# One more modulation unit summed on VectorE, attention transposes one step later, and the output norm written in pieces, in a two-layer fp32 diffusion step

## The chip, the cores and the metric

The kernel runs on one core of one Trainium2 chip. The metric is the device time of one execution in microseconds (us): the median of three runs is 2344.78 us, from 2342.45 to 2346.54. Matrix products run on TensorE (PE; its weight loads are shown as PEld), elementwise work on VectorE (DVE), activations and copies on ScalarE (ACT), a little on GpSimd (POOL); SyncE (SP) only issues transfers.

## The reference, cut to what matters

Two groups of 128 tokens, a prompt and a sample (256 columns in all), go through two layers with D = 2048. Each layer is a mixer and a gated MLP with a width-3 convolution, each behind a norm that is shifted, scaled and gated by six vectors per layer, which are themselves a product of a condition with a weight matrix (`w_ada`, 2048 by 12288 for each layer):

```python
def _trunk(x, cond, ...):
    for l in range(DEPTH):                                   # 2 layers
        mod = jax.nn.silu(cond) @ w_ada[l] + b_ada[l]        # (1, 6 * 2048)
        sh1, sc1, gt1, sh2, sc2, gt2 = jnp.split(mod[:, None, :], 6, axis=-1)
        h = rmsnorm(x, g_norm_mix[l]) * (1 + sc1) + sh1
        m, new = mixer_ab(h, ...) if l % 2 == 0 else mixer_c(h, ...)
        x = x + gt1 * m
        h = rmsnorm(x, g_norm_ffn[l]) * (1 + sc2) + sh2
        x = x + gt2 * conv_ffn(h, w_ffn_up[l], w_ffn_conv[l], b_ffn_conv[l], w_ffn_down[l])
    return rmsnorm(x, g_final), ab_ctx, c_ctx

def softmax_attention(q, k, v, scale):                       # 16 heads of mixer_ab: 8 "mla", 8 "gqa"
    s = jnp.einsum("bqhgd,bkhd->bhgqk", qb, k) * scale
    p = jax.nn.softmax(s, axis=-1)
    return jnp.einsum("bhgqk,bkhd->bqhgd", p, v)
```

The prompt group reads its own 128 keys, the sample group those and 128 cached ones. All is float32.

## The kernel before, in words

**Tokens lie in the columns**: `x` is 16 chunks of 128 features by 256 tokens and stays in SBUF for the whole run. The weights stream through once, in transfers of 1 MB into tiles called `raw` (three buffers) that SyncE issues in order. To multiply float32 data the kernel splits each weight into a rounded part `wh` (a cast on ACT, L222) and a rest `wl` (a subtraction on DVE, L223), and does the same to the activations. One 128x128 block is then three matmuls of 256 columns (L339 wh with the high part, L340 wh with the low part, L343 wl with the high part), which accumulate in a PSUM bank `acc` (three of them).

**The modulation vectors** are made beside this, from `w_ada`, which streams in tiles of 1 MB called `araw` (two buffers, also issued by SyncE). A unit (l, j, q) is a quarter (512 outputs) of vector j of layer l and takes four such tiles. The list `ROWS` gives the order of units. Most are done on TensorE (`sum_rows`, L453): for each tile four fp32 matmuls of 32x512, at the end a copy `am` on ACT (L395), four transposes (L402), a reduction on DVE (L404) and the bias (L412). Units whose index is in `SUMMED` are done on VectorE (`feature_sum`, L430): two multiplies with a sum over 128x2048 for each tile, eight for a unit; their products go to a `junk` tile that nobody reads, and their order against the work around them is fixed. A second list, `FEATS`, holds units that are always done on VectorE.

**The order** is written out as demands. After each chunk of weights `pump()` is called: it advances the list of units by a rate (`RATE`, `row_step`), and `step()` advances every attention head by one `yield`, since a head is a generator (`head_ab`). A scheduler then places each engine's instructions by its own estimates, within the dependencies.

**The stages by the trace**, in us from the start of the span: first norm and the input projection of the first mixer (0 to 211); its heads, with the query and key/value up-projections (211 to about 351); its output projection with the gated residual (L618; 351 to 447); MLP, second mixer, MLP (447 to 2330); last norm and output (2330 to 2343.7). In the heads a head is: scores (L666, into one of three banks `att`), softmax parts (maxima and scale on DVE, exponentials on ACT), scaling by the reciprocal (L674, L675), a yield, three transposes and the copy `pT` on ACT (`transposed`, L656 and L658), a yield, and the product with the values (L680 to L682), which is split into `hx` chunk c, the input of the output projection.

**A later norm** (`stat_add`, `stat_rstd`) is the tail of each stage: the residual of the last chunk on DVE (L618), its square on ACT (L173), two matmuls for each group (L202 on the sum of the other squares, L203 on the last square), a power on POOL (L189), a diagonal (L209) and its spread over the partitions by a matmul (L217). The last norm is followed by 16 multiplications (L1156) and four output transfers (L1159).

Of the kernel before, what the change touches and what calls it, by code (L numbers as in the profile page):

```python
# [12 lines left out]
BF16 = mybir.dt.bfloat16  # L13
AF = mybir.ActivationFunctionType
ALU = mybir.AluOpType
# [3 lines left out]
P = 128  # L19
# [59 lines left out]
FEATS += [(1, 5, 1), (1, 5, 2), (1, 5, 3)]  # L79
RLIMIT = {"ab": 18, "ffn0": 19, "c": 30, "ffn1": 31}  # L80
FLIMIT = {"ab": 2, "ffn0": 14, "c": 14, "ffn1": 17}
SUMMED = [20, 21, 22, 24, 25, 26, 29]
INV = {2048: 0, 768: 1, 512: 2, 128: 3, 256: 4}


# [1 line left out]
def step_kernel(ctx: ExitStack, tc: tile.TileContext, A: dict):  # L87
# [22 lines left out]
    def T_(pl, shape, tag, dt=F32, bufs=None):  # L110
        kw = {} if bufs is None else {"bufs": bufs}
        return pl.tile(shape, dt, tag=tag, name=nm(tag), **kw)
# [41 lines left out]
    def start(g):  # L154
        if next(g, chains) is not chains:
            chains.append(g)
# [8 lines left out]
    def stat_add(st, src, n):  # L165

        st["n"] += 1
        if st["n"] == 1:
            st["acc"] = T_(keep, [P, NT], "sqacc")
            act.activation(st["acc"], src, AF.Square)  # L170
            return
        sq = T_(tmp, [P, NT], "sq", bufs=2)
        act.activation(sq, src, AF.Square)  # L173
        if st["n"] == n:
            st["last"] = sq
        else:
            pool.tensor_tensor(out=st["acc"], in0=st["acc"], in1=sq, op=ALU.add)  # L177

    def rstd(cols, n, factor=1.0, out=None):
# [247 lines left out]
    def feature_sum(unit, t, c, raw, junk):  # L427

        l, j, q = unit
        tc.keep_in_program_order(dve.tensor_tensor_reduce(  # L430
            out=junk, in0=raw, in1=condb[:, c].rearrange("p (g n) -> p g n", g=4), scale=1.0, scalar=0.0,
            op0=ALU.mult, op1=ALU.add, accum_out=mod[:, l, j, 4 * q + t, c:c + 1]))
# [25 lines left out]
    def row_step(until=len(ROWS)):  # L458
        if later:
            later.pop(0)()  # L460
        if ada["i"] >= until:
            return
        l, j, q = ROWS[ada["i"]]
        if ada["i"] < 8:
            return pair_step(l, j, q)
        t, g = divmod(ada["t"], 4)
        on_dve = ada["i"] in SUMMED
        if g == 0:
            ada["raw"] = T_(wpool, [P, 4, 512], "araw", bufs=2)
            sp.dma_start(out=ada["raw"], in_=A["w_ada"][l, j, q, t])  # L470
        raw = ada["raw"]
        if on_dve:
            if g % 2:
                feature_sum((l, j, q), t, g // 2, raw, T_(ada["pool"], [P, 4, 512], "junk", BF16, bufs=1))
        elif pinned[0]:
            if g == 1 and t:
                sum_rows(t - 1, ada["last"])
            if g == 3:
                ada["last"] = raw
                if t == 3:  # L480
                    last = ada["last"]
                    later.append(lambda: None)
                    later.append(lambda: sum_rows(3, last))
        elif g == 3:
            sum_rows(t, raw)
        ada["t"] += 1
        if ada["t"] == 16:
            later.extend([lambda: biased(l, j, q)] if on_dve else ada_finish(l, j, q))
            ada["i"] += 1
            ada["t"] = 0  # L490
# [162 lines left out]
    def transposed(pl, p, bufs=2):  # L653
        pt = T_(ppool["att"], [P, 512], "att", bufs=3)
        for b in range(3):
            pe.transpose(pt[:, b * T:(b + 1) * T], p[:, b * T:(b + 1) * T], ident)  # L656
        o = T_(pl, [P, 3 * T], "pT", bufs=bufs)
        act.copy(o, pt[:, :3 * T])  # L658
        return o

    def head_ab(pl, pairs, rs, v, hx, c):

        s = T_(ppool["att"], [P, 512], "att", bufs=3)
        for g, ks in ((0, slice(0, T)), (1, slice(T, 3 * T))):
            for i, (q, k) in enumerate(pairs):
                pe.matmul(s[:, ks], q[:, g * T:(g + 1) * T], k[:, ks],  # L666
                          start=(i == 0), stop=(i == len(pairs) - 1))
        mx = T_(small, [P, 2], "mx")
        sums = T_(small, [P, 2], "sums")
        p = T_(pl, [P, 3 * T], "p", bufs=2)  # L670
        softmax_parts(s, mx, sums, rs, None, p)
        rec = T_(small, [P, 2], "rec")
        dve.reciprocal(out=rec, in_=sums)
        dve.tensor_scalar(out=p[:, :T], in0=p[:, :T], scalar1=rec[:, 0:1], scalar2=None, op0=ALU.mult)  # L674
        dve.tensor_scalar(out=p[:, T:], in0=p[:, T:], scalar1=rec[:, 1:2], scalar2=None, op0=ALU.mult)  # L675
        yield
        pT = transposed(pl, p)
        yield
        o = T_(ppool["att"], [P, 512], "att", bufs=3)
        pe.matmul(o[:, 0:T], v(0), pT[:, 0:T], start=True, stop=True)  # L680
        pe.matmul(o[:, T:NT], v(1), pT[:, T:2 * T], start=True, stop=False)
        pe.matmul(o[:, T:NT], v(2), pT[:, 2 * T:], start=False, stop=True)  # L682
        split(hx[:, c, :NT], hx[:, c, NT:2 * NT], o[:, :NT])


    def mixer_ab(hx, rb0, st):
        l = 0
        with tc.tile_pool(name="ab", bufs=1) as ab:
# [158 lines left out]

            with tc.tile_pool(name="abh", bufs=1) as hp:
                ada["pew"] = PEW["heads"]

                o = T_(keep, [P, KD, ROW], "hx", F32R)
                load_cw(0)
# [31 lines left out]
                for h in range(0, 8, 2):  # L884
                    for i in range(2):
                        ps = gemm(WQ.chunk(), qh, qlo)
                        qn[i] = T_(hp, [P, NT], "qn", bufs=3)
                        act.copy(qn[i], ps)
                        pump(RATE["heads"])
                    ps = gemm(WQ.chunk(), qh, qlo)  # L890
                    ev = T_(tmp, [P, NT], "nt", bufs=4)
                    act.copy(ev, ps)
                    qr = T_(hp, [P, NT], "qr", bufs=2)
                    act.copy(qr[:, 0:T], ev[:, 0:T])
                    rope(qr[:, None, T:], ev[:, None, T:], 1, 32, "rcm", "rsm")
                    pump(RATE["heads"])
                    kn = []
                    for i in range(2):
                        if h + i < 7:
                            start(gqa_query(h + i + 1))  # L900
                        start(gqa(h + i))
                        ps = gemm(WK.chunk(), kh, klo, 3 * T)
                        kn.append(T_(hp, [P, 3 * T], "kn", bufs=2))
                        act.copy(kn[i], ps)
                        pump(RATE["heads"])
                    wide = WK.pieces
                    WK.blocks = []
                    vm = T_(hp, [P, 3, 2, P], "vm", bufs=1)
                    vs = vm.rearrange("p b i d -> p (b i d)")
                    two, one = T_(pacc, [P, 512], "acc"), T_(pacc, [P, 512], "acc")  # L910
                    for xs, out in zip(tokens, (two[:, :NT], two[:, NT:], one[:, :NT])):
                        by_token(wide, xs, [out], True, True)
                    act.copy(vs[:, :2 * NT], two)
                    act.copy(vs[:, 2 * NT:], one[:, :NT])
                    pump(RATE["heads"])
                    start(mla(h, qn[0], qr, kn[0], vm))
                    pump(RATE["heads"])
                    start(mla(h + 1, qn[1], qr, kn[1], vm))
# [137 lines left out]
    def ffn(hx, W, ready, todo, l, st):  # L1056
# [4 lines left out]
        with tc.tile_pool(name=f"ffn{l}", bufs=1) as fp, banks(f"pffn{l}") as pf:  # L1061
# [38 lines left out]
            def down(gs, q):  # L1100
                for c in range(KD):
                    quiet = q == NQ - 1 and c >= KD - QUIET[0]
                    fine[0] = quiet
                    ps = gemm(WD.chunk(), lambda k: gs[k][:, :NT], lambda k: gs[k][:, NT:2 * NT])
                    residual(ps, l, 1, c, st if q == NQ - 1 else None)
                    pump(0, 0 if quiet else FRATE["down"])

            for q in range(NQ):
# [29 lines left out]
    ffn(hx, W, ready, todo, 0, st)  # L1138
    stage[0] = "c"
    with tc.tile_pool(name="cc", bufs=1) as cp, banks("pc") as ppool["ada"]:  # L1140
        ada["pool"] = cp
        ppool["att"] = ppool["ada"]
        W = Weights(A["w_in_c"], KD, 1)
        hx, ready, todo = modulated(st, 1, 0, W, True)
        load_cw(1)
        st = stat_init()
        ada["pew"] = PEW["c"]
        mixer_c(cp, hx, W, ready, todo, st)
        W = Weights(A["w_up"][1], KD, 1)
        hx, ready, todo = modulated(st, 1, 1, W, True)  # L1150
# [1 line left out]
    st = stat_init()  # L1152
    ffn(hx, W, ready, todo, 1, st)
    rb = norm_scale(st)
    for c in range(KD):
        dve.scalar_tensor_tensor(out=x[:, c], in0=x[:, c], scalar=C("gfin")[:, c:c + 1], in1=rb,  # L1156
                                 op0=ALU.mult, op1=ALU.mult)
        if c % 4 == 3:
            sp.dma_start(out=A["o_y"][:, c - 3:c + 1], in_=x[:, c - 3:c + 1])  # L1159

# [132 lines left out]
```

## Time and profile before

| | |
|---|---|
| median of three runs | 2344.78 us (2342.45 to 2346.54) |
| the profiled execution's own time | 2345.51 us |
| its span on the core | 2343.7 us |
| granted TensorE clock, mean | 0.993 of full speed |
| busy share of the span | PE 98%, DVE 78%, ACT 50%, POOL 6% |
| moved by DMA | 610.81 MB, 261 GB/s on average |

The span runs from the first to the last instruction of the core; what lies between it and the execution's own time is 1.8 us. PE is busy nearly throughout, so a time that is saved or added must show as PE work, as an idle stretch of PE, or at the two ends of the span, where PE has nothing to do.

### The profile page before, as it was taken

Reading aid. Unit: us, or ns where it says so; the run is one execution under the profiler, and the core shown is the slowest. Engines: PE = TensorE matmul, PEld = TensorE weight load, DVE = VectorE, ACT = ScalarE, POOL = GpSimd, SP = SyncE. Lnnn points to the kernel's source line nnn. Section 1 sums busy time; section 2 is a strip of 40 time slices with the busy share of each in tenths; the row PEclk is TensorE's granted clock in tenths of the full one; section 3 lists DMA queues with packets and bytes.
Section 4 is the critical chain, followed back from the end, with each engine's and each line's share of the span. In section 5 each row is a group of like instructions: output and inputs, shape, how many; then the busy total and the mean of one; then the engine's idle time right before and its main releaser. Section 6 shows DMA issues by size and latency. Waiting matters only on the chain. (4 is left out here: it accounts for less than half of the span.)

```text
span 2343.7 us, 47002 instructions
## 1 busy us (share of the span) xinstructions
PE 2295.5 (98%) x19582; PEld 2189.7 (93%) x19582; DVE 1817.6 (78%) x2692; ACT 1162.2 (50%) x1833; POOL 144.9 (6%) x133
## 2 busy tenths in 40 slices
PE   7999999999999999999999999999999999999997
PEld 6788878799999999999989999898999999999997
DVE  3667558879999999999869889887899755666654
ACT  4346554555553355554465555446555434555542
POOL 0002001200000000001220000022000000000011
PEclk9999999999999999999999999999999999999998
DMA  9996779777767777777767788786677555555553
GB/s 386 338 360 257 264 280 376 285 263 259 261 256 288 292 267 267 270 260 271 280 235 265 267 308 301 285 325 228 234 261 264 195 198 196 189 193 197 198 190 117
DMA packets 92421, 610.81 MB, mean 261 GB/s; under 512 B 9968, under 2 KB 17840, under 8 KB 20528
## 3 DMA queue, kind: packets, MB, share of 16 engines
q1 hardware_dynamic: 92208, 607.80, 70.3%
q8 instruction: 154, 2.52, 0.4%
q14 instruction: 59, 0.48, 0.1%
HBM read 603.01 MB, written 4.75 MB: 259 GB/s over the span
## 5 line engine op out<-in xcount | busy, mean ns | idle before, releaser
L222 ACT CAST wh<-raw 128x1024 fp32r<-128x1024 f32 (+1 forms) x788 | 793.2, 1012 | 936.6 <-PE acc L340 756.1
L223 DVE TENSOR_TENSOR wl<-raw,wh 128x1024 fp32r<-128x1024 f32 (+1 forms) x788 | 923.1, 1186 | 318.1 <-ACT wh L222 306.9
L339 PE MATMUL acc<-hx,wh 128*128 128x256 f32 x3808 | 1058.7, 279 | 6.3 <-ACT hx L569 4.6
L340 PE MATMUL acc<-hx,wh 128*128 128x256 f32 x3808 | 1055.9, 278 | 0.6 <-DVE hx L554 0.6
L343 PE MATMUL acc<-hx,wl 128*128 128x256 f32 x3808 | 1056.0, 278 | 0.0
L339 PEld LDWEIGHTS acc<-hx,wh 128*128 128x128 f32 x3808 | 716.0, 188 | 32.4 <-issue 9.2
L343 PEld LDWEIGHTS acc<-hx,wl 128*128 128x128 f32 x3808 | 716.0, 188 | 7.9 <-issue 6.7
L340 PEld LDWEIGHTS acc<-hx,wh 128*128 128x128 f32 x3808 | 716.8, 188 | 3.8 <-issue 2.6
L430 DVE CUSTOM_DVE_ANT_0 junk<-araw,condb 128x2048 f32<-128x2048 f32 (+1 forms) x192 | 442.9, 2307 | 0.1
L340 PE MATMUL acc<-g,wh 128*128 128x256 f32 x1408 | 388.3, 276 | 0.0
L343 PE MATMUL acc<-g,wl 128*128 128x256 f32 x1408 | 388.0, 276 | 0.0
L339 PE MATMUL acc<-g,wh 128*128 128x256 f32 x1408 | 387.8, 276 | 0.0
L340 PEld LDWEIGHTS acc<-g,wh 128*128 128x128 f32 x1408 | 264.3, 188 | 0.0
L343 PEld LDWEIGHTS acc<-g,wl 128*128 128x128 f32 x1408 | 264.2, 188 | 0.0
L339 PEld LDWEIGHTS acc<-g,wh 128*128 128x128 f32 x1408 | 264.1, 188 | 0.0
L177 POOL TENSOR_TENSOR sqacc<-sqacc,sq 128x256 f32<-128x256 f32 x62 | 84.9, 1369 | 1575.2 <-issue 1293.8
L1071 ACT ACTIVATE cv<-acc,convw 128x256 f32<-128x256 f32 x176 | 98.2, 558 | 1.4 <-PE acc L327 1.4
L618 DVE SCALAR_TENSOR_TENSOR x<-acc,mod,x 128x128 f32<-128x128 f32 x192 | 58.0, 343 | 42.5 <-PE acc L343 41.7
L1077 DVE SCALAR_TENSOR_TENSOR cv<-acc,convw,cv 128x254 f32<-128x254 f32 x176 | 84.3, 479 | 3.6
L1074 DVE SCALAR_TENSOR_TENSOR cv<-acc,convw,cv 128x254 f32<-128x254 f32 x176 | 83.5, 475 | 2.5 <-ACT cv L1071 2.5
L453 PE MATMUL ada<-araw,condw 128*32 128x512 f32 x512 | 68.6, 603 | 4.2 <-DMA araw<-w_ada 4.2
L304 PE MATMUL acc<-wh,hx 128*128 128x256 f32 x256 | 70.3, 281 | 0.9 <-ACT dv L982 0.9
(238 smaller groups left out, 2127.5 us busy)
## 6 DMA issues: line engine op xcount, KB each, us to landing
araw<-w_ada SPq DMA_DIRECT2D x178, 1024.0 KB, 5.5
raw<-w_up SPq DMA_DIRECT2D x176, 1024.0 KB, 4.8
raw<-w_down SPq DMA_DIRECT2D x88, 1024.0 KB, 4.8
raw<-w_in_c SPq DMA_DIRECT2D x48, 1024.0 KB, 5.6
raw<-w_in_ab SPq DMA_DIRECT2D x19, 1024.0 KB, 7.2
raw<-w_out_ab SPq DMA_DIRECT2D x16, 1024.0 KB, 7.4
raw<-w_out_c SPq DMA_DIRECT2D x16, 1024.0 KB, 6.0
condb<-w_ada SPq DMA_DIRECT2D x12, 1024.0 KB, 7.1
```

The costliest lines, as they stand in the source:

```text
L177: pool.tensor_tensor(out=st["acc"], in0=st["acc"], in1=sq, op=ALU.add)
L222: pin(act.copy(out_hi, src))
L223: pin(dve.tensor_tensor(out=out_lo, in0=src, in1=out_hi.bitcast(F32), op=ALU.subtract))
L304: pe.matmul(ps, hi, wh[:, s], start=a, stop=False)
L339: fixed(pe.matmul(ps[:, :n], wh, xh(k), start=(i == 0), stop=False))
L340: fixed(pe.matmul(ps[:, :n], wh, xl(k), start=False, stop=False))
L343: fixed(pe.matmul(ps[:, :n], wl, xh(k), start=False, stop=(i == last)))
L430: tc.keep_in_program_order(dve.tensor_tensor_reduce(out=junk, in0=raw, in1=condb[:, c].rearrange("p (g n) -> p g n", g=4), scale=1.0, scal ...
L453: i = pe.matmul(ada["ps"][32 * g:32 * g + 32, :], condw[:, 4 * t + g, :], raw[:, g], start=(t == 0), stop=(t == 3), skip_group_check=True)
L1071: pin(act.activation(y, ps, AF.Identity, scale=cw[:, 1, m:m + 1], bias=cw[:, 3, m:m + 1]))
L1074: pin(dve.scalar_tensor_tensor(out=y3[:, :, 1:], in0=p3[:, :, :T - 1], scalar=cw[:, 0, m:m + 1], in1=y3[:, :, 1:], op0=ALU.mult, op1=ALU.add))
L1077: pin(dve.scalar_tensor_tensor(out=y3[:, :, :T - 1], in0=p3[:, :, 1:], scalar=cw[:, 2, m:m + 1], in1=y3[:, :, :T - 1], op0=ALU.mult, op1=A ...
```

## The change

It has four parts.

1. Index 10 joins `SUMMED`: this is unit (0, 2, 2), a quarter of the first mixer's gate, whose four tiles are streamed while the heads run. Its eight sums are now done on VectorE. The heads have no space for a junk tile, so the products go to chunks 4 to 7 of `o`, which is the first mixer's `hx` and not yet written there (`ada["junk"]`, set to None at h = 4, before the first of those heads starts). The unit's weights come transposed, as those of the other units in `SUMMED` do.
2. `head_ab` has one more `yield` ahead of `transposed`: in all 16 heads the transposes of the attention weights come one demand later, and what follows them too.
3. At the end, the multiplication by `g_final` moves into the last down-projection, as an activation with a scale on ACT after each chunk's residual; what is left after the norm are five multiplications of 2, 4, 4, 4 and 2 chunks, each followed by its own output transfer, in place of 16 and four.
4. The last square of each norm behind the first stage (three of them: ahead of the second mixer, ahead of the second MLP, and at the end) is done in two halves, one for each group of tokens.

```diff
-SUMMED = [20, 21, 22, 24, 25, 26, 29]
+SUMMED = [10, 20, 21, 22, 24, 25, 26, 29]
@@ stat_add
         sq = T_(tmp, [P, NT], "sq", bufs=2)
-        act.activation(sq, src, AF.Square)
         if st["n"] == n:
+            for s in ([slice(0, NT)] if stage[0] == "ab" else [slice(0, T), slice(T, NT)]):
+                act.activation(sq[:, s], src[:, s], AF.Square)
             st["last"] = sq
         else:
+            act.activation(sq, src, AF.Square)
             pool.tensor_tensor(out=st["acc"], in0=st["acc"], in1=sq, op=ALU.add)
@@ row_step
-                feature_sum((l, j, q), t, g // 2, raw, T_(ada["pool"], [P, 4, 512], "junk", BF16, bufs=1))
+                feature_sum((l, j, q), t, g // 2, raw, ada["junk"]())
@@ head_ab
         yield
+        yield
         pT = transposed(pl, p)
         yield
@@ the heads
                 ada["pew"] = PEW["heads"]
+                ada["junk"] = lambda: o[:, 4:8]
...
                     pump(RATE["heads"])
+                    if h == 4:
+                        ada["junk"] = None
                     start(mla(h, qn[0], qr, kn[0], vm))
@@ down
                     residual(ps, l, 1, c, st if q == NQ - 1 else None)
+                    if l == 1 and q == NQ - 1:
+                        act.activation(x[:, c], x[:, c], AF.Identity, scale=C("gfin")[:, c:c + 1])
                     pump(0, 0 if quiet else FRATE["down"])
@@ the second mixer
-        ada["pool"] = cp
+        ada["junk"] = lambda: T_(cp, [P, 4, 512], "junk", BF16, bufs=1)
@@ the end
     rb = norm_scale(st)
-    for c in range(KD):
-        dve.scalar_tensor_tensor(out=x[:, c], in0=x[:, c], scalar=C("gfin")[:, c:c + 1], in1=rb,
-                                 op0=ALU.mult, op1=ALU.mult)
-        if c % 4 == 3:
-            sp.dma_start(out=A["o_y"][:, c - 3:c + 1], in_=x[:, c - 3:c + 1])
+    for c, n in ((0, 2), (2, 4), (6, 4), (10, 4), (14, 2)):
+        dve.tensor_tensor(out=x[:, c:c + n], in0=x[:, c:c + n], op=ALU.mult,
+                          in1=rb[:, None, :].to_broadcast([P, n, NT]))
+        sp.dma_start(out=A["o_y"][:, c:c + n], in_=x[:, c:c + n])
```

Line numbers after the change are higher by two behind `stat_add`, and by up to seven towards the end (L430 becomes L432, L656 L658, L666 L668, L680 L683).

Two places in the heads show what moves. The first is VectorE in the first quarter of the heads, around a head's softmax (its `p` scaled by L674 and L675) and the next pieces of split weights (`wl`). Before:

```order
L673 RECIPROCAL rec_2593<-sums_2585 128x2
L674 TENSOR_SCALAR p_2586<-p_2586,rec_2593 128x128
L675 TENSOR_SCALAR p_2586<-p_2586,rec_2593 128x256
L223 TENSOR_TENSOR hx_2381<-att_2612,hx_2381 128x256
L223 TENSOR_TENSOR wl_2789<-raw_2782,wh_2788 128x512
L404 TENSOR_REDUCE mod_77<-ada_2571 128x8
L412 TENSOR_TENSOR mod_77<-mod_77,cst_74 128x8
L223 TENSOR_TENSOR wl_2887<-raw_2884,wh_2886 128x1024
L223 TENSOR_TENSOR wl_2891<-raw_2884,wh_2890 128x1024
```

And the same place after:

```order
L677 TENSOR_SCALAR p_2582<-p_2582,rec_2589 128x256
L432 ISA hx_2381,mod_77<-araw_2502,condb_82 128x2048
L432 ISA mod_77 128x1
L225 TENSOR_TENSOR wl_2769<-raw_2762,wh_2768 128x512
L225 TENSOR_TENSOR hx_2381<-att_2669,hx_2381 128x256
L644 TENSOR_REDUCE mx_2690<-att_2685 128x1
L645 TENSOR_REDUCE mx_2690<-att_2685 128x1
L406 TENSOR_REDUCE mod_77<-ada_2566 128x8
L649 SCALAR_TENSOR_TENSOR nmx_2693<-mx_2690,rsmla_240 128x2
L414 TENSOR_TENSOR mod_77<-mod_77,cst_74 128x8
L432 ISA hx_2381,mod_77<-araw_2502,condb_82 128x2048
L432 ISA mod_77 128x1
```

Two of the eight sums (each is an instruction of 128x2048 and a short one that writes its result) now stand there, the first ahead of the pieces of weights `wl` and the second ahead of the next ones; the maxima of the next head, which came later, stand between them.

The second place is TensorE ahead of the second pair of heads' value up-projection (the `L304` product; `L306` after). Before:

```order
L680 MATMUL att_3036<-pT_2987,vg_236 128x128
L681 MATMUL att_3036<-pT_2987,vg_236 128x128
L682 MATMUL att_3036<-pT_2987,vg_236 128x128
L453 MATMUL ada_2860<-araw_2989,condw_79 32x512 x4
L666 MATMUL att_3050<-kn_2907,qn_2762 128x128
L666 MATMUL att_3050<-kr_233,qr_2851 128x128
L666 MATMUL att_3050<-kn_2907,qn_2762 128x256
L666 MATMUL att_3050<-kr_233,qr_2851 128x256
L867 MATMUL misc_3637<-cst_74,sq_3593 128x1 x2
L402 MATMUL ada_3074<-cst_74,am_3048 128x128 x4
L304 MATMUL acc_3370<-wh_3253,kv_in_231 128x256
```

After:

```order
L658 MATMUL att_2943<-cst_74,p_2856 128x128 x3
L683 MATMUL att_3007<-pT_2947,vg_236 128x128
L684 MATMUL att_3007<-pT_2947,vg_236 128x128
L685 MATMUL att_3007<-pT_2947,vg_236 128x128
L658 MATMUL att_3013<-cst_74,p_2917 128x128 x3
L668 MATMUL att_3027<-kn_2890,qn_2750 128x128
L668 MATMUL att_3027<-kr_233,qr_2828 128x128
L668 MATMUL att_3027<-kn_2890,qn_2750 128x256
L668 MATMUL att_3027<-kr_233,qr_2828 128x256
L455 MATMUL ada_2843<-araw_2903,condw_79 32x512 x4
L683 MATMUL att_3045<-pT_3017,vg_236 128x128
L684 MATMUL att_3045<-pT_3017,vg_236 128x128
```

Two heads' transposes (`L658`) have come to this place, out of the key up-projection ahead of it, and each stands close before the product (`L683` and on) that needs its copy; the transposes of a modulation unit (`L402`) have left it. Row for row, GpSimd's order is as before, and SyncE's differs only in the heads and the output projection, where tiles `araw` and `raw` alternate in another order, and in the last five transfers.

## Prediction

> **What bounds the kernel now.** I read first the busy shares, then windows by stage, then what TensorE waits for in the stages that the change touches, last the timeline of the end. The page's first part, then two answers of windows (after the colon-separated stretch and its length: busy us of PE, PEld, DVE, ACT and POOL with their instructions, granted clock, DMA share, GB/s):
>
> ```profile
> PE 2295.5 (98%) x19582; PEld 2189.7 (93%) x19582; DVE 1817.6 (78%) x2692; ACT 1162.2 (50%) x1833; POOL 144.9 (6%) x133
> ```
>
> ```profile
> 0.00:211.00 211.00, 195.17 (x1566) 162.15 (x1567) 120.83 (x243) 98.87 (x181) 19.42 (x25) 0.98 0.87 335
> ...
> 447.00:2330.00 1883.00, 1866.00 (x16163) 1832.28 (x16162) 1529.26 (x2096) 952.78 (x1427) 100.44 (x85) 1.00 0.68 247
> ```
>
> ```profile
> 229.50:280.00 50.50, 50.50 (x391) 41.61 (x391) 28.36 (x81) 27.70 (x65) 2.96 (x4) 1.00 0.72 266
> 280.00:351.00 71.00, 68.65 (x521) 54.45 (x522) 33.94 (x102) 34.68 (x85) 1.38 (x2) 1.00 0.74 271
> 351.00:447.00 96.00, 94.67 (x804) 83.23 (x802) 83.81 (x108) 38.12 (x56) 17.70 (x14) 1.00 0.88 349
> ```
>
> TensorE is the bound, at full granted clock. In the heads' first part (229.5 to 280) it never idles, in the second it idles 71.00 − 68.65 = 2.35 us, in the output projection 1.33. VectorE is busy for 28.36 of 50.5 us in the first part. So PE work taken out of the heads comes off the span one for one, as long as nobody else becomes late. What PE waits for in the heads, and from 320 on (total, times, longest):
>
> ```profile
> PE acc L339 <- ACT qn L888: 1.0, 1, 1.0
> PE att L680 <- ACT pT L658: 0.6, 1, 0.6
> ```
>
> ```profile
> PE ada L453 <- DMA araw<-w_ada: 1.3, 1, 1.3
> ```
>
> The same wait of 0.6 stands in both answers, at two places: a value product whose copy `pT` is not ready.
>
> **The sum goes against the profiled execution**: 2345.51 us, of which the span is 2343.7. That is 0.73 us above the median 2344.78, so gains are taken from 2345.51 and the median is placed by the same difference. About 0.2% of the time, 4.7 us, is what a measurement of this kernel can tell from no change.
>
> **Part 1a, the unit leaves TensorE.** A piece of the chain of waits in a saturated stretch shows a tile's eight records (four matmuls of two each) and four transposes as they displace other products; the timeline of the heads shows them as well:
>
> ```profile
> 1628.45 0.99 PE misc L453 x8
> 1629.44 0.32 PE acc L343
> 1629.76 0.12 PE acc L339
> ...
> 1635.10 0.44 PE misc L402 x4
> ```
>
> ```profile
> 242.18 1.92 PE L453 MATMUL ada<-araw,condw 128*32 128x512 f32 x16
> ...
> 253.02 1.06 PE L453 MATMUL ada<-araw,condw 128*32 128x512 f32 x8
> ```
>
> Four tiles and one set of transposes: 4 × 0.99 + 0.44 = 4.4 us. Two tiles in one go take 1.92, which gives 2 × 1.92 + 0.44 = 4.3; with the slower first product behind a tile (0.32 in place of 0.12) it is 4.4 + 4 × 0.2 = 5.2. I take 4.4.
>
> **Part 1b, VectorE gets eight sums.** The second mixer's and MLP's sums are of the same shape:
>
> ```profile
> L223 DVE TENSOR_TENSOR wl<-raw,wh 128x1024 fp32r<-128x1024 f32 x713 | 871.5, 1235 | 298.5 <-ACT wh L222 287.5 <-PE acc L340 4.9 <-PE misc L453 0.3
> L430 DVE CUSTOM_DVE_ANT_0 junk<-araw,condb 128x2048 f32<-128x2048 f32 x120 | 274.7, 2289 | 0.0
> ```
>
> Eight take 8 × 2.289 = 18.3 us. All eight fall among the pieces of the stretch from 229.5 to 280, because their order is fixed there, ahead of weight pieces `wl` and of the softmax's scalings. VectorE then has 28.36 + 18.3 = 46.7 us of work, in a stretch that TensorE would finish in 50.5 − 4.4 = 46.1. So VectorE, which had 22 us of slack, is level with TensorE. If it never idles it is 0.6 us late at the end. It does idle, since it waits for casts and scores. The fullest stretch in which TensorE still loses nothing to it:
>
> ```profile
> 650.00:700.00 50.00, 50.00 (x443) 50.00 (x442) 47.13 (x61) 26.21 (x37) 0.00 (x0) 1.00 0.70 254
> ```
>
> There VectorE is busy for 47.13 of 50 us, 94%. At that share it needs 46.7 / 0.94 = 49.7 us, 3.6 late. I take 2.0 us of new waits of TensorE, between 0.6 and 3.6: the pieces that the sums push back are split ahead of their use, but the scalings of a head's `p` are not, and PE's transposes wait for those. The bounds are 0 (all slack found, the last pieces used only later) and 7.4: in the output projection VectorE is full, at 83.81 of 96 us, or 87%, and 46.7 / 0.87 is 53.5. The am copy and its reduction leave ACT and VectorE, 0.19 us on the latter, which I leave out. The junk lands in chunks that heads 4 to 7 write later, behind the sums on the same engine or long after them: nothing.
>
> The queue of SyncE carries `araw` and `raw` in one order. A tile's buffer comes free two sums after its landing instead of four matmuls, and a `raw` tile behind it waits as well. With two `araw` buffers and a landing in 5.4 us (quoted below), I count nothing beyond the 2.0; the other case is a rival.
>
> **Part 2, transposes one demand later.** In the heads there are three places where a head's transposes stand directly ahead of its value product, so that the copy between lies open; in the new order there is one.
>
> ```profile
> L658 ACT COPY pT<-att 128x384 f32<-128x384 f32 x24 | 11.5, 478 | 26.0 <-PE att L656 25.9
> ```
>
> The copy's 0.478 us shows as the wait of 0.6, so two places fewer are 1.2 us. As many instructions run as before. The other idle time of the heads (2.35 in all) may go too: it depends on VectorE's scalings, which are later now by a sum here and there. I take 1.0, between 0 and 2.4.
>
> **Part 4, halves of the last square.** The end of the last norm, and the same place ahead of the second mixer:
>
> ```profile
> 2328.96 0.61 DVE L618 SCALAR_TENSOR_TENSOR x<-acc,mod,x 128x128 f32<-128x128 f32 x2 [6.87 <-PE acc L343]
> 2329.67 0.42 ACT L173 ACTIVATE sq<-x 128x256 f32<-128x256 f32 x1 [7.06 <-DVE x L618]
> ...
> 2330.14 0.38 PE L203 MATMUL misc<-cst,sq 128*128 128x1 f32 x2 [1.10 <-ACT sq L173]
> ...
> 2331.00 0.16 DVE L185 TENSOR_SCALAR rv<-misc 128x2 f32<-128x2 f32 x1 [1.43 <-PE misc L203]
> ```
>
> ```profile
> 1179.44 1.04 ACT L222 CAST wh<-raw 128x1024 fp32r<-128x1024 f32 x1 [1.68 <-PE acc L340]
> 1179.50 0.61 DVE L618 SCALAR_TENSOR_TENSOR x<-acc,mod,x 128x128 f32<-128x128 f32 x2 [0.48 <-PE acc L343]
> 1180.39 0.41 ACT L173 ACTIVATE sq<-x 128x256 f32<-128x256 f32 x1
> ```
>
> All of this lies open: PE has nothing else. The first half's square can run under the second half's residual, and the first group's two products then run ahead of the second square; 0.46 of the 0.86 us from 2330.14 to 2331.00 goes, and about 0.1 of the square. At the end that is 0.5. Ahead of the mixer the square waits for a cast, not for the residual, so two halves cost about 0.2 more on ACT and 0.46 − 0.2, about 0.3, is left. Two such norms: 0.6. Bounds: 0, if a half costs as much as the whole 0.41 (that eats the 0.46; more it cannot take, since the first group's products go ahead in any case), and 1.0, the end's 0.5 twice.
>
> **Part 3, the end.** Then 16 multiplications, which send four pieces:
>
> ```profile
> 2333.84 6.36 DVE L1156 SCALAR_TENSOR_TENSOR x<-x,cst,misc 128x256 f32<-128x256 f32 x16 [1.38 <-PE misc L217]
> 2335.52 5.03 SPq L1159 DMA_DIRECT2D o_y<-x  x4
> ```
>
> ```profile
> q1 hardware_dynamic: 576, 2.10, 38.3%
> issues: line engine op xcount, KB each, median us to landing
> o_y<-x SPq DMA_DIRECT2D x4, 512.0 KB, 2.6
> ```
>
> (The second view covers 2330 to 2343.7, 13.7 us.) The transfers take 38.3% of 13.7 = 5.2 us, 1.3 for each 512 KB. The last is issued at about 2340.2 and lands 2.6 later, at 2342.8. Five multiplications last, by the elementwise rows of their size, 3 × 1.235 and 2 × 0.721 (a row of 128x512 elements):
>
> ```profile
> L223 DVE TENSOR_TENSOR wl<-raw,wh 128x512 fp32r<-128x512 f32 x73 | 49.8, 721 | 19.6 <-ACT wh L222 19.4
> L223 DVE TENSOR_TENSOR g<-cv,g 128x256 fp32r<-128x256 f32 x88 | 36.6, 416 | 0.9 <-ACT g L222 0.9
> L809 DVE TENSOR_TENSOR proj<-proj,acc 128x256 f32<-128x256 f32 x60 | 24.6, 418 | 20.0 <-PE acc L343 19.6
> ```
>
> (An operand from PSUM costs nothing more: 418 against 416 ns.) That is 5.1 us, 4.8 with four overlaps of 0.08, in place of 6.36, and the first piece is issued 0.72 in place of 1.68 behind the start. From there the transfers bind: start 2333.84 − 0.5 (Part 4) + 0.72 = 2334.06, then 2.6 − 1.3 = 1.3 until bytes move, then 5.2 of bytes: 2340.6. That is 2.2 earlier; I take 2.0, of which 0.5 are the halves. Bounds: 0.6, if a smaller piece costs as much as a big one, and 2.6, if the last piece only takes its bytes' 0.65.
>
> The Trainium skill, "DMA: Bandwidth & Descriptors", section "Anatomy of one DMA — SWDGE (gpsimd) path", gives a transfer a fixed cost of about 2.0 us beside its bytes at 436 GB/s, for another queue than this; taken one after the other, five pieces would be an estimated 14.8 us and four 12.8, and the end 2 us longer. The trace speaks against the series: four pieces are issued about 1.57 us apart and each lands in 2.6, so fixed parts overlap.
>
> The 16 multiplications by `g_final` go to ACT:
>
> ```profile
> L1071 ACT ACTIVATE cv<-acc,convw 128x256 f32<-128x256 f32 x176 | 98.2, 558 | 1.4 <-PE acc L327 1.4
> ```
>
> ```profile
> 1480.00:2330.00 850.00, 841.90 (x7334) 826.09 (x7332) 602.96 (x826) 417.17 (x585) 50.41 (x43) 1.00 0.61 219
> ```
>
> 16 × 0.558 = 8.9 us on an engine half idle (417 of 850 us); the last one runs behind the square, under products on PE and POOL. Nothing; without that cover 0.56.
>
> **The sum**: 4.4 − 2.0 + 1.0 + 0.6 + 2.0 = 6.0 us. Span 2337.7, the profiled run's own time 2339.5, the median 2338.8.
>
> **The rivals.** *VectorE binds in the heads.* By the 87% above, PE waits 7.4 us in place of 2.0, and of 6.0 there is left 0.6: 2344.2. For it: 46.7 us of work in 46.1. Against it: weights are split ahead.
>
> *Slower: SyncE's queue stops.* An `araw` transfer waits for VectorE to free a buffer, and weight tiles stand behind it. The landing (from 205 to 320):
>
> ```profile
> araw<-w_ada SPq DMA_DIRECT2D x20, 1024.0 KB, 5.4
> ```
>
> If two weight tiles are late by one landing, 10.8 us of PE waits come to the 2.0: 6.0 − 10.8 = −4.8, 2349.6. It decides when a pair of sums ends more than the raw tiles' lead after its tile landed. Against it: DMA is only 0.72 busy in that stretch.
>
> *The end pays for pieces.* If each piece's 1.3 us ahead of its bytes is paid in turn, the fifth takes 1.3 of the 2.0: gain 4.7, 2340.1.
>
> *No new wait.* VectorE's sums fit into its slack and all 2.4 us of old waits go: 4.4 + 2.4 + 0.6 + 2.0 = 9.4, 2335.4.
>
> **How the numbers follow.** Forecast 0.48, VectorE bound 0.22, queue stops 0.10, pieces dear 0.08, no new wait 0.12. Faster by more than 4.7 us are the last (0.12), the forecast save for its edge (0.41) and a little of the pieces (0.02): 0.55. Within are VectorE's case (0.19), the rest of the pieces (0.06) and the forecast's edge (0.07): 0.32. Slower are the queue and a worse VectorE: 0.13. The range goes from no new wait, 2335.4, to VectorE's case with the end's low bound (1.4 less): 2345.6. Left out are the queue and the outer edges.
>
> **What would show it.** Right: between 229 and about 276 VectorE busy for 46 us or more; PE's products there in 46 to 48 us; in the heads fewer waits for `pT`, some for the scaled `p` or `wl`; the second L203 behind its own square; five o_y transfers that end 2 us sooner after the last residual. Wrong: PE waits of over 4 us in the heads for VectorE (the first rival), `raw` landing late there (the second), o_y issues in which each starts only as the last one lands (the third).

## The result, and the profile after

The changed kernel takes 2339.49 us in the median of seven runs (2337.12 to 2341.60), the kernel before 2346.54 in seven of its own. The ratio is 0.9972, with a 95% interval from 0.9962 to 0.9981: 6.6 us faster (4.5 to 8.9). Forecast were 6.0 us, and 2338.8 us. The total was right. Two of its main terms were not, as the experiments show.

The windows of the changed kernel by stage (columns as in the prediction), from its profiled run of 2337.97 us:

```profile
229.50:280.00 50.50, 48.74 (x372) 43.17 (x364) 45.51 (x101) 28.21 (x66) 6.87 (x6) 1.00 0.70 262
280.00:351.00 71.00, 69.34 (x539) 54.50 (x536) 32.66 (x99) 33.83 (x85) 0.00 (x0) 1.00 0.79 299
351.00:436.00 85.00, 84.17 (x714) 75.25 (x713) 80.58 (x101) 35.03 (x50) 21.62 (x14) 1.00 0.92 360
sum 206.50, PE 202.25 PEld 172.92 DVE 158.75 ACT 97.07 POOL 28.48; mean PE 67.42 PEld 57.64 DVE 52.92 ACT 32.36 POOL 9.49
```

In the first part of the heads VectorE (the third number with a count) is now busy for 45.51 of 50.5 us, from 28.36, and TensorE, which never idled there, idles 1.76. The last line adds the three stretches up: TensorE idles 206.50 − 202.25 = 4.25 us. The same sum of before:

```profile
sum 206.50, PE 202.82 PEld 169.85 DVE 140.56 ACT 97.17 POOL 20.16; mean PE 67.61 PEld 56.62 DVE 46.85 ACT 32.39 POOL 6.72
```

That is 3.68 us. So TensorE does not wait less than before, it waits elsewhere (in a second profile of the changed kernel it idles 4.9 us). The list of what it waits for in these stretches of the changed kernel shows whom for (total, times, longest):

```profile
PE att L683 <- ACT pT L660: 1.3, 2, 0.7
PE ada L455 <- DMA araw<-w_ada: 1.0, 2, 0.6
PE acc L345 <- DVE wl L225: 0.8, 1, 0.8
PE ada L455 <- DVE scl L419: 0.6, 1, 0.6
PE acc L341 <- ACT qn L892: 0.5, 1, 0.5
```

The waits for `pT` and `qn` lie in the first part of the heads, those for `araw` and `scl` (the scale of a norm) in the second, that for `wl` in the output projection. None is for the scaled `p` itself.

The end of the changed kernel, from the timeline:

```profile
2323.64 0.61 DVE L620 SCALAR_TENSOR_TENSOR x<-acc,mod,x 128x128 f32<-128x128 f32 x2 [6.87 <-PE acc L345]
2324.08 0.51 ACT L175 ACTIVATE sq<-x 128x128 f32<-128x128 f32 x2 [6.26 <-DVE x L620]
...
2325.31 0.16 DVE L187 TENSOR_SCALAR rv<-misc 128x2 f32<-128x2 f32 x1 [1.06 <-PE misc L205]
...
2326.91 0.67 PE L219 MATMUL misc<-diag,cst 128*128 128x256 f32 x2 [1.64 <-DVE diag L211]
2327.62 4.68 DVE L1164 TENSOR_TENSOR x<-x,misc 128x512 f32<-128x512 f32 x5 [0.85 <-PE misc L219]
2328.33 4.32 SPq L1166 DMA_DIRECT2D o_y<-x  x5
```

From the last residual to the end of the span it is 2336.2 − 2323.64 = 12.6 us, against 2343.7 − 2328.96 = 14.7: 2.2 sooner in these two profiles. The norm's first step (L187) stands 1.67 us behind the residual, where it was 2.04. The spread over the partitions (L219) takes 0.67 in place of 1.19, which is not the change's doing, as the last section shows.

### The profile page after: what moved, and what is told of

Its sections match the earlier page's. It is cut to its first block, busy times and chain, and to the rows that moved or that the text cites. A ratio compares the mean times of both kernels' runs of the same rounds, so it can differ in the third digit from the quotient of the medians.

```text
span 2336.2 us, 46935 instructions
## 1 busy us (share of the span) xinstructions
PE 2289.7 (98%) x19546; PEld 2187.6 (94%) x19546; DVE 1830.9 (78%) x2696; ACT 1169.7 (50%) x1851; POOL 152.4 (7%) x133
## 5 line engine op out<-in xcount | busy, mean ns | idle before, releaser
L432 DVE CUSTOM_DVE_ANT_0 junk<-araw,condb 128x2048 f32<-128x2048 f32 (+1 forms) x192 | 441.1, 2297 | 0.1
L306 PE MATMUL acc<-wh,hx 128*128 128x256 f32 x256 | 70.3, 281 | 0.9 <-ACT dv L988 0.9
L307 PE MATMUL acc<-wh,hx 128*128 128x256 f32 x256 | 70.1, 280 | 0.0
```

The source lines that it names most:

```text
L306: pe.matmul(ps, hi, wh[:, s], start=a, stop=False)
L307: pe.matmul(ps, lo, wh[:, s], start=False, stop=False)
L432: tc.keep_in_program_order(dve.tensor_tensor_reduce(out=junk, in0=raw, in1=condb[:, c].rearrange("p (g n) -> p g n", g=4), scale=1.0, scal ...
```

## The experiments

Each was timed in five rounds beside the kernel before on the same chip; the gains in us are the ratio times 2346.

The windows above are cut at fixed times, and the heads begin up to 3.3 us apart in the profiles. A steadier measure, called the stretch below, runs from one instruction to another: from the last sums of squares of the input projection (four products `misc<-cst,sq`, at 206.64 before) to the spread of the norm behind the output projection (L217, or L219; at 449.39 before). It holds the heads and the output projection. Before, all but the unit (see below), and two profiles of the changed kernel:

```profile
206.64:449.39 242.75, 237.64 (x1894) 199.07 (x1892) 165.83 (x352) 114.99 (x232) 26.13 (x24) 1.00 0.80 306
207.24:444.80 237.56, 236.51 (x1894) 199.41 (x1893) 164.86 (x352) 114.13 (x232) 32.62 (x24) 1.00 0.82 312
205.65:444.74 239.09, 233.74 (x1858) 198.12 (x1856) 180.85 (x367) 114.32 (x231) 33.34 (x24) 1.00 0.81 311
207.46:446.97 239.51, 233.49 (x1859) 197.65 (x1857) 180.57 (x367) 114.27 (x231) 33.38 (x24) 1.00 0.82 310
```

The first number behind the times is the stretch's length, the second TensorE's busy time. The two other kernels with the heads of before (the end alone, the halves alone) have 242.62 and 242.77, so differences of a microsecond can be told.

**The unit alone** (the diff's part 1 on the kernel before).

```diff
-SUMMED = [20, 21, 22, 24, 25, 26, 29]
+SUMMED = [10, 20, 21, 22, 24, 25, 26, 29]
...
+                ada["junk"] = lambda: o[:, 4:8]
```

> The kernel before with part 1 alone (the unit's sums on VectorE, no later transposes). If the parts simply add: 4.4 us of TensorE work gone, about 2 us of new waits for VectorE, gain 2 to 3 us. If the later transposes are needed for it (rival): the scaled p comes behind a sum, the transposes wait one demand early, and the gain falls under 1 us or turns to a loss of 1 to 3 us, with PE waits for p in the first heads.

Ratio 1.0009 (1.0000 to 1.0018): 2.1 us slower (0 to 4.2). TensorE idles 206.50 − 196.73 = 9.8 us in the three stretches, 6.1 more than before, and it waits for the scaled `p`:

```profile
sum 206.50, PE 196.73 PEld 165.57 DVE 152.88 ACT 96.01 POOL 23.30; mean PE 65.58 PEld 55.19 DVE 50.96 ACT 32.00 POOL 7.77
```

```profile
PE att L656 <- DVE p L674: 3.7, 2, 2.9
PE att L680 <- ACT pT L658: 1.8, 3, 0.6
PE ada L453 <- DMA araw<-w_ada: 1.7, 1, 1.7
```

The stretch is 246.6 us, 3.9 longer than before. The rival held: without the later transposes the unit costs more than it saves.

**The later transposes alone** (part 2).

```diff
         yield
+        yield
         pT = transposed(pl, p)
```

> The kernel before with part 2 alone (transposes one demand later). Additive theory: the two open pT copies of 0.6 us go, gain 0.5 to 1.2 us, no new waits. Rival: the later yield is only of use with the sums, and alone moves nothing (within 0.5 us) or costs, because attention banks are held longer.

Ratio 0.9978 (0.9969 to 0.9987): 5.2 us faster (3.0 to 7.3). Neither theory had that. TensorE's sum says where it comes from:

```profile
sum 206.50, PE 206.50 PEld 175.00 DVE 144.08 ACT 98.25 POOL 27.50; mean PE 68.83 PEld 58.33 DVE 48.03 ACT 32.75 POOL 9.17
```

It does not idle once, so all 3.7 us of the old waits are gone, those for `qn` and for `araw` (1.0 and 1.3) with those for `pT`. The stretch is 237.58 us, 5.2 shorter than before, as the times say; TensorE's busy time in it is also 1.1 less. Why the waits for `qn` and `araw` went too was not shown. One line of the kernel brings most of the gain.

**The end alone** (part 3).

```diff
-        dve.scalar_tensor_tensor(out=x[:, c], in0=x[:, c], scalar=C("gfin")[:, c:c + 1], in1=rb,
...
+    for c, n in ((0, 2), (2, 4), (6, 4), (10, 4), (14, 2)):
```

> The kernel before with part 3 alone (end by pieces, g_final on ACT). By the sum of the prediction the end is 1.5 us sooner, from the last residual to the last instruction 13.2 us in place of 14.7. The rival of dear pieces gives 0.2 us. ACT's 16 multiplications cost nothing elsewhere: the last down-projection starts and ends within 0.2 us of where it was, relative to the stage before.

Ratio 0.9995 (0.9986 to 1.0004): too small for the comparison. The timeline measures it better:

```profile
2328.31 0.61 DVE L618 SCALAR_TENSOR_TENSOR x<-acc,mod,x 128x128 f32<-128x128 f32 x2 [6.87 <-PE acc L343]
2330.34 0.16 DVE L185 TENSOR_SCALAR rv<-misc 128x2 f32<-128x2 f32 x1 [1.43 <-PE misc L203]
...
2333.18 4.68 DVE L1158 TENSOR_TENSOR x<-x,misc 128x512 f32<-128x512 f32 x5 [1.38 <-PE misc L217]
```

With a span of 2341.7 it is 13.4 us from the last residual to the end, 1.3 less than before, with the same slow spread in both (1.38 us of VectorE's idle time in front of the multiplications). The rival of dear pieces (0.2) falls; the five multiplications take 4.68, forecast 4.8.

**The halves alone** (part 4).

```diff
+            for s in ([slice(0, NT)] if stage[0] == "ab" else [slice(0, T), slice(T, NT)]):
+                act.activation(sq[:, s], src[:, s], AF.Square)
```

> The kernel before with part 4 alone (last square in halves). By the sum: 0.5 us at the end and 0.3 at each of two norms, 1.1 us in all. Rival: ACT's two halves cost as much as is gained at the two middle norms, and only the end's 0.4 to 0.5 is left.

Ratio 0.9998 (0.9990 to 1.0007), again inside the noise. At the end the halves take 0.37 us off, the 2.04 against 1.67 above, in this kernel as in the changed one. At a middle norm, here in the changed kernel, there is nearly nothing to gain:

```profile
1174.66 1.04 ACT L224 CAST wh<-raw 128x1024 fp32r<-128x1024 f32 x1 [1.68 <-PE acc L342]
1174.72 0.61 DVE L620 SCALAR_TENSOR_TENSOR x<-acc,mod,x 128x128 f32<-128x128 f32 x2 [0.48 <-PE acc L345]
1175.61 0.50 ACT L175 ACTIVATE sq<-x 128x128 f32<-128x128 f32 x2
...
1176.88 0.15 DVE L187 TENSOR_SCALAR rv<-att 128x2 f32<-128x2 f32 x1
```

Both halves stand behind the cast, and the first step comes 2.16 us behind the residual. Before, it was 2.22 (1179.50, and this row):

```profile
1181.73 0.16 DVE L185 TENSOR_SCALAR rv<-att 128x2 f32<-128x2 f32 x1
```

That is 0.06 us, not 0.3; the norm ahead of the second MLP shows the same (2.15 against 2.22). The rival held.

**All but the unit** (parts 2, 3 and 4).

```diff
-SUMMED = [10, 20, 21, 22, 24, 25, 26, 29]
+SUMMED = [20, 21, 22, 24, 25, 26, 29]
...
```

> The changed kernel without part 1 (the unit back on TensorE; later transposes, end and halves as changed). The prediction's theory (the unit is worth 4.4 - 2.0 us): 2.4 us slower than the changed kernel, a gain of 4 us over before. The theory from the single runs (the unit's 4.4 us are eaten by new waits, the later transposes carry the gain): within 1 us of the changed kernel, a gain of 6.5 to 8 us over before, with no idle time of TensorE in the heads.

Ratio 0.9967 (0.9956 to 0.9978): 7.7 us faster than before (5.2 to 10.3). The changed kernel, timed a second time beside the kernels of the last experiment, had 0.9966 (0.9953 to 0.9979), and 0.9972 at first. So by the times the unit brings nothing that can be told, either way by up to some 3 us, and TensorE without it does not idle:

```profile
sum 206.50, PE 206.50 PEld 175.01 DVE 143.78 ACT 98.06 POOL 27.45; mean PE 68.83 PEld 58.34 DVE 47.93 ACT 32.69 POOL 9.15
```

The stretch tells more: with the unit it is 1.5 and 1.9 us longer (239.09 and 239.51 against 237.56). TensorE has 36 records fewer in it (four tiles of eight and four transposes), is busy for 2.8 and 3.0 us less, and idles 4.3 and 5.0 us more. In this kernel the unit costs more than it saves, and the theory from the single runs held.

**Half of each sum, and each sum twice** (both on the changed kernel).

```diff
-            if g % 2:
+            if g % 2 and ada["i"] == 10:                                                     # half
+                tc.keep_in_program_order(dve.tensor_tensor_reduce(
+                    out=ada["junk"]()[:, 0:2], in0=raw[:, 0:2], ...
...
-                feature_sum((l, j, q), t, g // 2, raw, ada["junk"]())
+                for _ in range(2 if ada["i"] == 10 else 1):                                  # twice
+                    feature_sum((l, j, q), t, g // 2, raw, ada["junk"]())
```

> The changed kernel, but each of the unit's eight sums runs over 128x1024 in place of 128x2048 (half of each sum is left out, so the gate's quarter is incomplete). VectorE has about 9 us less to do in the heads, all else stays. If VectorE's time makes the new waits: the waits of the first heads go, and it is 2 to 4 us faster than the changed kernel. Rival (the waits come from the weights' transfers or buffers): within 0.7 us of the changed kernel.

> The changed kernel with each of the unit's eight sums done twice into the same place: 17.7 us more on VectorE in the heads, nothing more on TensorE. If VectorE is full there (46 us of work in 46): nearly all of it shows, 12 to 17 us slower than the changed kernel. If it still has room (the prediction's slack): under 6 us.

Half sums (a kernel that leaves out half of each sum): ratio 0.9948 (0.9936 to 0.9960), 12.2 us faster than before. Double sums: 1.0081 (1.0048 to 1.0115), 19.0 us slower. By the ratios half sums are 5.6 us faster than the changed kernel (more than the 2 to 4 expected), for 8.6 us less of VectorE (eight sums of 1.22 us in place of 2.28). The double sums' times lie far apart (2355.55 to 2386.11 us); the profiled run's span, 2353.8 us, is the shortest of them and 17.6 longer than the changed kernel's (12 to 17 were expected for a full engine), for 17.7 us more of VectorE. TensorE's sums, half and then double:

```profile
sum 206.50, PE 205.46 PEld 176.65 DVE 153.68 ACT 99.71 POOL 23.38; mean PE 68.49 PEld 58.88 DVE 51.23 ACT 33.24 POOL 7.79
```

```profile
sum 206.50, PE 195.35 PEld 166.81 DVE 162.91 ACT 93.99 POOL 23.79; mean PE 65.12 PEld 55.60 DVE 54.30 ACT 31.33 POOL 7.93
```

```profile
PE att L659 <- DVE p L677: 8.7, 3, 7.5
```

Idle 1.0 us with half sums, 11.2 with double ones, of which the scaled `p` has 8.7. VectorE's time makes the waits: the stretch is 234.61 us with half sums, 4.5 and 4.9 shorter than the changed kernel's two, and 248.31 with double ones, 9.2 and 8.8 longer. So about half of the 17.7 us come out in the stretch itself. Of the rest, TensorE waits 3.0 us for `hx` on VectorE and 3.4 for `cv` on ACT at the start of the MLP, where the changed kernel waits 0.8; why these are late was not shown, and neither was that VectorE's time comes out one for one.

**Another unit, in the emptier part of the heads** (unit 12 in place of 10, with chunks 6 and 7 as the place of products from h = 4 on).

```diff
-SUMMED = [10, 20, 21, 22, 24, 25, 26, 29]
+SUMMED = [12, 20, 21, 22, 24, 25, 26, 29]
...
+                        ada["junk"] = lambda: o[:, 6:8].bitcast(BF16).rearrange(...)   # from h == 4 to 6
```

> The changed kernel with unit 12 in place of unit 10 on VectorE: its sums fall in the second part of the heads, where VectorE is busy for about half of the time; the products go to chunks 6 and 7 as bf16. If VectorE's room decides: few new waits, 2.5 to 4.4 us faster than the changed kernel. Rival (a sum ahead of a head's softmax delays it wherever it stands): within 1 us of the changed kernel or slower.

Ratio 0.9991 (0.9983 to 1.0000): 2.1 us faster than before, 4.5 slower than the changed kernel by the ratios; the stretch, 242.54 us, is 3.5 and 3.0 longer than the changed kernel's two. The busy share of the second part does not show why:

```profile
280.00:351.00 71.00, 63.94 (x477) 54.17 (x477) 49.94 (x121) 33.93 (x79) 5.06 (x3) 0.95 0.66 248
```

VectorE is busy for only 50 of 71 us, yet TensorE idles 7.1:

```profile
PE att L658 <- DVE p L676: 5.4, 1, 5.4
PE ada L455 <- DMA araw<-w_ada: 1.1, 1, 1.1
```

VectorE's timeline ahead of that wait, which ends at 315.49 (rows left out are weights, rotations, another head's scaling of `p` at 307.44, and the next head's maxima):

```profile
298.87 2.29 DVE L432 CUSTOM_DVE_ANT_0 hx<-araw,condb 128x2048 fp32r<-128x2048 f32 x1
...
303.69 2.28 DVE L432 CUSTOM_DVE_ANT_0 hx<-araw,condb 128x2048 fp32r<-128x2048 f32 x1
...
309.03 2.28 DVE L432 CUSTOM_DVE_ANT_0 hx<-araw,condb 128x2048 fp32r<-128x2048 f32 x1
...
315.06 0.28 DVE L676 TENSOR_SCALAR p<-p,rec 128x128 f32<-128x128 f32 x1
```

Three sums and the work between them fill 16 us without a gap of over 0.1 us ahead of one head's `p`. What decides here is the queue ahead of that operation, not the share of a stage. The rival held.

**Room on VectorE, by GpSimd and by ACT** (on the changed kernel: the queries' rotation to GpSimd; the scaling of `p` to ACT; both).

```diff
-                    rope(qb[:, h:h + 1, T:], qb[:, h:h + 1, T:], 1, 64, "rch", "rsh")
+                    rope(qb[:, h:h + 1, T:], qb[:, h:h + 1, T:], 1, 64, "rch", "rsh", pool, hp)
...
-        dve.tensor_scalar(out=p[:, :T], in0=p[:, :T], scalar1=rec[:, 0:1], scalar2=None, op0=ALU.mult)
-        dve.tensor_scalar(out=p[:, T:], in0=p[:, T:], scalar1=rec[:, 1:2], scalar2=None, op0=ALU.mult)
+        act.activation(p[:, :T], p[:, :T], AF.Identity, scale=rec[:, 0:1])
+        act.activation(p[:, T:], p[:, T:], AF.Identity, scale=rec[:, 1:2])
```

> The changed kernel with the rotation of the eight grouped queries' heads (four multiplications and adds of 64x128 or 128x128 each time, about 1.7 us of VectorE for a head) on GpSimd, which is 7% busy, in a tile of its own. If VectorE's fullness is what eats the unit's gain: VectorE has some 7 to 8 us less in the first half of the heads, the new waits shrink as with half sums, 2 to 4 us faster than the changed kernel. Rival: GpSimd is so slow, or disturbs VectorE so much, that the scores wait for the rotated queries: same or slower.

> The changed kernel with the scaling of p by the reciprocal on ACT (two activations with a scale, about 1 us for a head) in place of two operations of VectorE (0.6 us for a head); VectorE has about 2.5 us less in the first half of the heads, and p no longer stands behind a sum on VectorE. If it is the scaled p that PE waits for: 1 to 3 us faster than the changed kernel. Rival: the reciprocal still stands behind the sums, and ACT's casts come later: within 1 us or slower.

> Both of the former in one kernel. If VectorE is the limit in the heads: no idle time of TensorE for VectorE is left in the heads, 3.5 to 5 us faster than the changed kernel. Otherwise as the worse of the two.

> The changed kernel once more, beside the three others: 6 to 7 us faster than before, as measured.

Beside the changed kernel at 2338.87 us (five runs): the rotation on GpSimd 2339.49 (ratio to before 0.9977, 0.9968 to 0.9987), the scaling on ACT 2334.35 (0.9948, 0.9936 to 0.9961), both 2334.26 (0.9949, 0.9935 to 0.9962). The first part of the heads, rotation on GpSimd and then scaling on ACT:

```profile
229.50:280.00 50.50, 48.67 (x356) 42.50 (x356) 43.81 (x88) 28.85 (x68) 23.91 (x30) 0.97 0.67 247
```

```profile
229.50:280.00 50.50, 50.30 (x389) 45.63 (x386) 43.70 (x94) 33.54 (x83) 7.51 (x5) 1.00 0.76 270
```

VectorE is equally busy in both, 43.8 and 43.7 us, yet TensorE idles 1.8 us in the first and 0.2 in the second. With the rotation on GpSimd it waits for `p`, which stands behind the sums:

```profile
PE att L658 <- DVE p L676: 1.1, 1, 1.1
```

With the scaling on ACT no wait for `p` stands in the list; the changed kernel's list has none either, but there a sum can stand between a head's reciprocal and its `p` (reciprocal at 255.52, sum at 257.26, `p` at 259.47), and the transposes stand close ahead of their product (262.46 and 264.02), so that the copy between lies open. Over the whole stretch the rotation's move takes 6.3 us off VectorE (174.59 in place of 180.85), and the length stays (239.37 us). The scaling's move takes 8.4 off it (172.45), and the stretch is 5.4 and 5.8 us shorter than the changed kernel's two (233.68). Both together take 14.5 off and bring no more than the scaling alone (233.73). So this speaks for the place of one operation and against the amount of VectorE's time. What the rotation's move may lose by itself was not separated: GpSimd takes 742 ns for a piece of 64x128 for which VectorE took 292, and VectorE's own operations take longer beside it. With GpSimd busy, then in the changed kernel (229 to 280, groups by form):

```profile
L432 DVE CUSTOM_DVE_ANT_0 hx<-araw,condb 128x2048 fp32r<-128x2048 f32 x8 | 18.7, 2336 | 1.2 <-DMA araw<-w_ada 1.2
...
L635 DVE TENSOR_TENSOR rope<-nt,cst 32x128 f32<-32x128 f32 x8 | 2.8, 352 | 2.0 <-ACT nt L896 1.8
```

```profile
L432 DVE CUSTOM_DVE_ANT_0 hx<-araw,condb 128x2048 fp32r<-128x2048 f32 x8 | 18.3, 2284 | 1.9 <-DMA araw<-w_ada 1.9
...
L635 DVE TENSOR_TENSOR rope<-nt,cst 32x128 f32<-32x128 f32 x8 | 2.3, 283 | 0.2
```

That is 352 against 283 ns and 2336 against 2284.

The kernel with the scaling on ACT, with or without the rotation on GpSimd, is the fastest complete one here: 12.2 us faster than before (9.1 to 15.0), and by the medians 4.5 faster than the changed one, more than the 1 to 3 expected (the two intervals of the ratio overlap by 0.0008). For the rotation alone the rival held.

## Why the prediction was right, point by point

The total came out, and so did the sum for the heads and the output projection: forecast 4.4 − 2.0 + 1.0 = 3.4 us, and the stretch is 3.2 to 3.7 us shorter. In its parts this is luck: the unit, forecast to bring 2.4, costs 1.5 to 1.9, and the later transposes, forecast to bring 1.0, bring 5.2. The two errors are in opposite directions and about as large.

- **TensorE loses 4.4 us of work**: not shown as a number. The unit's 36 records are gone, but TensorE's busy time in the stretch falls by only 2.8 to 3.0 us, and by 5.1 in the kernel with the scaling on ACT, which waits little. Where TensorE waits, its other products take longer in sum; why was not followed up.
- **New waits, 2.0**: mis-sized, 4.3 to 5.0 against the kernel without the unit. The 1.76 us in the first part of the heads are near the forecast, but they are waits for the copy `pT` and for `qn`, not for the scaled `p`. Left out were 1.66 in the second part and 0.83 in the output projection, for `araw`, `scl` and `wl`, 60 us and more behind the last sum; half sums leave 1.0 us of these 2.5, but how they hang on the sums was not shown. The step that failed is the reading of VectorE's share: 94% without loss was taken from the MLP, and a share does not show what stands ahead of a head's `p`.
- **Later transposes, 1.0, at most 2.4**: mis-sized, 5.2 (3.0 to 7.3), outside the stated bounds. Alone, they took away both waits for `pT`, as counted. What failed is the rest of the term: the waits for `qn` (1.0) and `araw` (1.3) went too, the latter in the output projection, which the bound did not count, and TensorE's busy time fell by 1.1. In the changed kernel two waits for `pT` stand again, at other places, where one open copy was forecast.
- **The middle norms, 0.6**: 0.1. Both halves wait for the same cast.
- **The end, 2.0**: 1.7, 1.3 by pieces and 0.37 by halves.
- **The rival of VectorE as the bound** priced the waits at 7.4; the truth lies between it and the forecast. *SyncE's queue* showed as waits for `araw`, 1.0 us in all in one profile of the changed kernel and 2.0 in the other, not 10.8. *Dear pieces*: from the last issue to the end of the span it is 3.9 us with five pieces and 3.5 with four, 0.4 and not 1.3.
- **The signs**: VectorE was to be busy for 46 us or more between 229 and about 276; it is busy for 42.0 of these 47 us. Fewer waits for `pT` did not show (1.3 us in place of 1.2), nor one for the scaled `p`; the one for `wl` (0.8) lies in the output projection. The order of the last squares and the five transfers came as said.

By the runs the sum reads 5.2 for the later transposes, less 1.5 to 1.9 for the unit, and 0.1 + 1.7: 5.1 to 5.5 us, beside 6.6 measured (4.5 to 8.9).

## What to carry to other kernels

Work moved from a full engine to one with room can cost more than it saves when something that the full engine waits for stands behind it: look at the queue ahead of that one operation, not at the busy share of the stage. Compare stages from one instruction to the same instruction, not between fixed times, since a stage's start moves from run to run. Where several small waits stand between two engines, a longer distance between producer and consumer (a later step in a software pipeline) may take them all away at once, and is worth trying before anything is moved. A combined change should be taken apart even if its total comes out as forecast: here one part carried the gain and another cost some of it.

## What the runs showed of the hardware that was not expected

The same spread ahead of the output, two matmuls of 128x256 after 1.64 us in which TensorE had nothing to do, takes 1.19 us in three of the fourteen profiles (before, the end alone, all but the unit) and 0.67 in the eleven others, with and without the halves. The windows of before and of the changed kernel around it:

```profile
2332.55:2333.85 1.30, 1.19 (x2) 0.50 (x2) 0.01 (x1) 0.00 (x0) 0.00 (x0) 0.50 0.00 0
```

```profile
2326.85:2327.65 0.80, 0.67 (x2) 0.30 (x2) 0.03 (x1) 0.00 (x0) 0.00 (x0) 0.95 0.00 0
```

The granted clock was 0.50 in the first and 0.95 in the second. At the norm behind the output projection it differs as well between two kernels whose rows are the same there up to 452.3 (later transposes alone, all but the unit):

```profile
440.00:460.00 20.00, 17.23 (x108) 11.41 (x107) 17.92 (x49) 14.07 (x35) 6.00 (x8) 0.74 0.68 263
```

```profile
440.00:460.00 20.00, 17.24 (x121) 11.42 (x120) 17.92 (x49) 14.07 (x35) 6.02 (x8) 0.83 0.68 263
```

The Trainium skill, "TensorE: Matmul & The Clock Gate", in "Part 1: The HAM clock gate", has TensorE's clock at half rate after an idle window of about 3.4 us, judged in windows that run freely, so that the point of change differs between executions. The trace agrees with the half rate and with the difference between executions; but before the slow spread the gaps were of 1.1 and 1.6 us, each under the 3.4. That these windows are the cause was not shown here.

0.74 against 0.83 over 20 us is 1.8 us of full clock. The first MLP starts at the same time in both (449.15 and 449.14), but its products start 0.21 us apart until about 455.5 in the first and 452.5 in the second, and 0.11 apart from then on; the next modulation tile behind them comes 1.4 us later in the first (461.69 against 460.25). So a gap of TensorE can cost more than its idle time, by an amount that changes from run to run, and a part of the change that is worth less than 2 us can be read only from a timeline. The profiled run of before had the slow spread and that of the changed kernel the fast one: 0.5 of the 2.2 us at the end in these two profiles is that.
